# Two constants of a list scheduler, and 64- and 96-row operands of TensorE filled to 128 rows

## The chip, the cores and the metric

One core of a Trainium2 chip runs the program. The metric is the device time of one execution in microseconds; several executions were timed, and one more was recorded by the hardware profiler.

## The reference

Two blocks run one after the other on 512 tokens of width 1024, all in float32. The first has two layers, and each is a feed-forward, a mixer and a feed-forward:

```python
x = x + 0.5 * swiglu(rmsnorm(x, ffn1_norm[l]), ffn1_wg[l], ffn1_wu[l], ffn1_wd[l])
h = rmsnorm(x, mix_norm[l]) @ w_in[l]
h_a, h_b, h_c = jnp.split(h, [A_COLS, A_COLS + B_COLS], axis=-1)
o = jnp.concatenate([mla_mixer(h_a, ...), nsa_mixer(h_b, ...), diff_mixer(h_c, ...)], axis=-1)
x = x + o @ w_out[l]
x = x + 0.5 * swiglu(rmsnorm(x, ffn2_norm[l]), ...)
```

`mla_mixer` has six heads of 64 + 32 channels whose queries and keys come from low-rank factors (192 and 128 wide); the 32 channels are turned by position (rope). `nsa_mixer` has six heads with compressed, selected and windowed keys; its q and three kinds of k get a partial rope. `diff_mixer` has four heads that subtract two softmaxes, with rope on q and k of 32 channels. The second block is a gated recurrence beside a dilated attention, then a mixture of 16 experts, each taking 64 tokens through three 1024x1024 matrices.

## The kernel before

The kernel is not written in the order in which it runs. A `Recorder` takes down every operation with its alternatives (a copy or a small elementwise operation may go to one of two or three engines); a list scheduler then walks through planned time, hands each engine the ready operation of highest priority, gives out the eight PSUM banks, and emits each engine's row of instructions in that order. Its planned lengths come from `duration` (a formula for each engine and operation) and, for TensorE, from `pe`, which goes through the products of one operation and carries `weights`: the last weights, and which 64-column half of the array the last product used. All emitted instructions stand under one line of the profile, L500, so the trace is read by shapes and times.

Float32 accuracy comes from splitting operands into a high and a low float32r part; a product of two such operands is three passes (high x high, high x low, low x high). Loads of weights run on SyncE's queue; splitting the loaded weights is a CAST and a TENSOR_TENSOR of 128x1024 on DVE, ACT or POOL.

A mixer runs in this order as recorded: `group` products for columns "a", then `mla_prep`; the groups "qk", "kv", "cqk" (the differential heads' q and k, 512 columns) and "cv" (their values, 256 columns); `mla_heads`; and then `nsa_prep`, `diff_prep` and the heads of these two. The scheduler mixes them: the large products of the groups fill TensorE while softmaxes of `mla_heads` pass through DVE and ACT, and the ropes of `nsa_prep` run on DVE and POOL. Below, arena_126 is a half of the cv weights as loaded, arena_128 and arena_129 its high and low part; arena_150 and arena_151 are NSA's q and k, arena_153 its doubled k, arena_269 to arena_276 the four terms of a rope, arena_119 and arena_120 the cosine and sine, arena_92 the identity matrix of a transpose.

Operands with fewer than 128 rows are these: `w2l`, the low part of the last 64 rows of the query factor (`mla_prep`, `mla_heads`: 64 rows, where the contraction runs over 64 rows); `QP` and `KP`, the rope channels of MLA as 3 x 32 rows; and `cqk`, the differential heads' q and k, also 3 x 32 rows.

Of the kernel before, what the change touches and what calls it, by code (L numbers as in the profile page):

```python
# [31 lines left out]
       ("ACT", "POOL"): 159, ("DVE", "ACT"): 128, ("DVE", "PE"): 202, ("DVE", "POOL"): 155, ("POOL", "ACT"): 75,  # L32
       ("POOL", "DVE"): 70, ("POOL", "PE"): 149, ("ACT", "ACT"): 34, ("DVE", "DVE"): 127, ("POOL", "POOL"): 102,
       ("PE", "PE"): 0, ("SP", "SP"): 0}
TABLES = {AF.Exp: 1, AF.Silu: 2, AF.Sigmoid: 3, AF.Sin: 4}


# [39 lines left out]
class Recorder:  # L77
# [390 lines left out]
    def pe(self, calls, t, weights):  # L468
        for _, m, a, k in calls:
            out, st, mov = a[0], a[1], a[2]  # L470
            key = (st.tensor.name, st.offset, tuple(st.ap))
            half = out.ap[0][1] == 64 and (out.offset % SPAN) // (512 * 64)
            d = duration("PE", m, a, k)
            if key == weights[0] and st.dtype != F32:
                d = free(mov) / 2.4 + 2.5
            if out.ap[0][1] == 64 and weights[1] is not None and weights[1] == 1 - half:

                d, half = 57, None
            elif out.ap[0][1] != 64:
                half = None  # L480
            t, weights = t + d, (key, half)
        return t, weights
# [35 lines left out]
def duration(eng, m, a, k):  # L518
    aps = [x for x in list(a) + list(k.values()) if is_ap(x)]
    out = k.get("out", a[0] if a else None)  # L520
    if m == "dma_start":
        src = k.get("in_", a[1] if len(a) > 1 else None)
        n = 1
        for c in src.shape:
            n *= c
        return n * 4 / 395.0
    if eng == "PE":
        st, mov = a[1], a[2]
        if m == "transpose":
            return 109.0  # L530
        n, mm = free(mov), free(st)
        if st.dtype == F32:
            return 2 * max(n / 1.2 + 2, 53.0 if mm <= 64 else 107.0)
        return max(n / 2.4 + 2.5, 56.0 if st.dtype == BF else 107.0)
    n = max(free(x) for x in aps)
    ps = any(x.space == PSUM for x in aps)
    if eng == "ACT":
        d = (51 if ps else 93) + 0.834 * n
        if m == "activation":
            d += 93 * (is_ap(k.get("scale")) or is_ap(k.get("bias"))) + 93 * ("accum_out" in k)  # L540
        return d
    if eng == "DVE":
        if m in ("tensor_copy", "memset"):
            return 65 + 1.042 * n if ps else 69 + 0.52 * n
        if m in ("tensor_scalar", "tensor_scalar_mul", "tensor_scalar_add"):
            return (65 + 1.042 * n if ps else 69 + 0.52 * n) + 60 * any(is_ap(x) for x in a[2:])
        if m == "scalar_tensor_tensor":
            return 73 + 1.157 * n
        if m == "reciprocal":
            return 69 + 6.25 * n  # L550
        return 68 + 1.042 * n
    if m in ("memset", "iota", "affine_select"):
        return 100 + 0.834 * n
    if m == "tensor_scalar":
        return 243 + 46 * sum(is_ap(x) for x in a[2:]) + 0.834 * n
    if m == "tensor_scalar_mul":
        return 260 + 3.33 * n
    if m == "tensor_copy":
        return 121 + 3.33 * n
    return 126 + 2.123 * n  # L560
# [62 lines left out]
T = 512  # L623
# [10 lines left out]
def r32(ap):  # L634
    return ap.bitcast(F32R)
# [228 lines left out]
class Mixer:  # L864
# [145 lines left out]
    def tr4(self, src, pool, bufs=2):  # L1010
# [5 lines left out]
            self.nc.tensor.transpose(ps[:r, 128 * c:128 * c + 128], p, self.ident)  # L1016
        return ps[:r]

    def three(self, x):

        return f32(x.rearrange("p a b -> p (a b)"))
# [82 lines left out]
    def mla_prep(self, l, ap, pr, pp, ha):  # L1104
# [10 lines left out]
            q(wkv[:, :768].rearrange("p (h r c) -> p h r c", h=6, r=2)[:, :, r], ukv[:, :, :64])  # L1115
        q(wkv[:, 768:].rearrange("p (h c) -> p h c", h=6), ukv[:, :, 64:])
        w1h, w2h, wkvh = (ap.tile([128, n], F32R, name=m) for m, n in (("w1h", 576), ("w2h", 576), ("wkvh", 1152)))
        w1l, w2l, wkvl = r32(w1), r32(w2[:64]), r32(wkv)
        self.split_sb(w1h, w1l, w1)
        self.split_sb(wkvh, wkvl, wkv)  # L1120
        self.copy(w2h, w2)
        self.tt("tensor_sub", w2l, w2[:64], f32(w2h[:64]))
        sc = 96 ** -0.5

        ss, rr = (ap.tile([128, 2, 4], F32, name=n) for n in ("ss", "rr"))
# [10 lines left out]
        hl = pr.tile([128, 4, 3, 32], F32R, name="kst")  # L1136
        self.copy(hl[:, :, :2], kpe[:, :, None].to_broadcast([128, 4, 2, 32]))
        self.tt("tensor_sub", hl[:, :, 2], kpe, f32(hl[:, :, 0]))
        KP = ap.tile([96, T], F32R, name="KP")
        self.copy(KP, self.tr4(lambda c: self.three(hl[:, c]), pp))  # L1140
        for tb in range(4):
            self.scaled(ha[:, tb, :192], ha[:, tb, :192], rr[:, 0, tb:tb + 1])
            self.scaled(ha[:, tb, 192:320], ha[:, tb, 192:320], rr[:, 1, tb:tb + 1])
# [13 lines left out]
        for c2_ in range(2):  # L1157
            ps = pp.tile([128, T], F32, name="s", bufs=2)
            for c in range(2):
                tok = slice(128 * (2 * c2_ + c), 128 * (2 * c2_ + c) + 128)  # L1160
                out, r = ps[:, 192 * c:192 * c + 192], slice(384, 576)
                for n, (x, w) in enumerate(((c1h, w1h), (c1h, w1l), (c1l, w1h), (c2, w2h), (c2[:64], w2l))):
                    mm(out, x[:, tok], w[:, r], start=c == 0 and n == 0, stop=n == 4, skip_group_check=True)
            self.scaled(qpe[:, 2 * c2_:2 * c2_ + 2], ps[:, :384].rearrange("p (c h d) -> p c h d", c=2, h=6), sc)
        self.rope(qpe, 6, 16, pr)
# [13 lines left out]
    def mla_heads(self, e, mp, pp, oa):  # L1179
# [4 lines left out]
        for p in range(3):  # L1184
            ps = pp.tile([128, T], F32, name="pq", bufs=1)
            w = lambda n: e[n][:, 128 * p:128 * p + 128]
            for n, (a, x) in enumerate((("w1h", "c1h"), ("w1h", "c1l"), ("w1l", "c1h"), ("w2h", "c2"), ("w2l", "c2"))):
                mm(ps, w(a), e[x][:64] if n == 4 else e[x], start=n == 0, stop=n == 4)
            Q = [self.stack2(mp, ps, x, "Q", 2, sc) for x in range(2)]
            passes = []  # L1190
            for x in range(2):
                h = 2 * p + x
                ps = pp.tile([128, T], F32, name="pq", bufs=1)
                for n, (a, c) in enumerate((("wkvh", "ch"), ("wkvh", "cl"), ("wkvl", "ch"))):
                    mm(ps, e[a][:, 128 * h:128 * h + 128], e[c], start=n == 0, stop=n == 2)
                KH, KL, QP = (mp.tile([r, T], F32R, name=n, bufs=2) for n, r in (("KH", 128), ("KL", 128), ("QP", 96)))
                self.split_out(KH, KL, ps)
                ps = self.tr4(lambda c: self.three(e["hq"][:, c, h]), pp)
                self.copy(QP, ps)
                passes.append([(Q[x], KH), (Q[x], KL), (QP, e["KP"])])  # L1200
            av = pp.tile([128, T], F32, name="av", bufs=2)
            for i in (3, 2, 1, 0):
                pt = self.turned(st, [self.softmax(st, i, passes[x]) for x in range(2)], i + 1)
                self.outputs(av, i, i + 1, pt, lambda x, j: e["V"][:, j, 2 * p + x, :], i == 3, True)
            self.split_out(*oa[p], av)
# [28 lines left out]
    def diff_heads(self, l, lam, hl, V, dp, mp, pp, oc):  # L1234
# [4 lines left out]
        for p in range(2):  # L1239
            passes = []  # L1240
            for h in (2 * p, 2 * p + 1):
                w = []
                for c in range(2):
                    qk = []
                    for s in range(2):
                        t = mp.tile([96, T], F32R, name="cqk", bufs=8)
                        self.copy(t, self.tr4(lambda tb: self.three(hl[s][:, tb, 2 * h + c]), pp))
                        qk.append(t)
                    w.append([tuple(qk)])
                passes.append(w)  # L1250
# [942 lines left out]
```

## Time and profile before

| what | value |
|---|---|
| median of 3 executions | 2970.51 us (2967.53 to 2972.78) |
| the profiled execution's own time | 2972.06 us |
| its span in the trace | 2970.3 us |
| mean granted TensorE clock | 0.993 of full speed |
| PE busy | 2894.5 us, 97% |
| DVE, ACT, POOL busy | 56%, 21%, 9% |

The span runs from the first to the last recorded instruction; the profiled execution's own time has 1.8 us around it. The stages on the time axis are: first feed-forward to about 365 us; first mixer 365 to 745; two feed-forwards 745 to 1412; second mixer 1412 to 1790; last feed-forward to 2090; the second block's mixer to about 2490; the experts from there to the end.

### The profile page before, as it was taken

How to read it: one execution, taken by the hardware profiler on the slowest of the kernel's cores; microseconds unless marked ns; L12 is line 12 of the kernel's file. 1: busy time of each engine (PE TensorE's matmuls, PEld its weight loads, DVE VectorE, ACT ScalarE, POOL GpSimd, SP SyncE). 2: the span in 40 equal slices, each digit the busy share in tenths (PEclk: the TensorE clock that was granted, in tenths of full speed). 3: DMA queues.
4: the chain of work that ended last, by engine and by line, in shares of the span. 5: the costliest groups of instructions: out<-in, count | busy, mean ns of one | idle time of the engine just before them, and what ended most of it. 6: DMA issues, size and time to landing. Idle time of an engine off the chain costs nothing.

```text
span 2970.3 us, 37457 instructions
## 1 busy us (share of the span) xinstructions
PE 2894.5 (97%) x14909; PEld 2192.1 (74%) x14909; DVE 1669.2 (56%) x3051; ACT 634.0 (21%) x1364; POOL 279.2 (9%) x279
## 2 busy tenths in 40 slices
PE   9999999999999999999999999999999999999998
PEld 7888877777888888888777778888777876444443
DVE  6554565886555455555658865555767783311212
ACT  3000133472000010001334721001222361100000
POOL 1000111211000010001112210000223120000000
PEclk9999999999999999999999999999999999999999
DMA  4333322102333333333221023333312356999999
GB/s 124 99 93 98 109 78 62 47 5 77 90 100 99 97 89 100 100 96 112 78 60 56 2 78 90 95 96 100 89 57 71 100 179 242 384 409 409 409 409 349
DMA packets 273139, 403.61 MB, mean 136 GB/s; under 512 B 34809, under 2 KB 210982, under 8 KB 272966
## 3 DMA queue, kind: packets, MB, share of 16 engines
q1 hardware_dynamic: 272806, 401.09, 40.1%
q8 instruction: 117, 1.92, 0.3%
q14 instruction: 56, 0.46, 0.0%
q0 software_dynamic: 160, 0.14, 0.0%
HBM read 399.09 MB, written 2.10 MB: 135 GB/s over the span
## 4 chain that ended last, share of the span: by engine, by line
PE 87%; DVE 8%; DMA 3%; issue 1%; ACT 1%; POOL 1%; SPq 0%; DVEq 0%; POOLq 0%; ACTq 0%
PE bank L500 87%; DVE arena L500 8%; DMA arena<-in_w_expert_up 1%; ACT arena L500 1%; DMA arena<-in_ffn_wd 1%; POOL arena L500 1%; DMA arena<-in_w_expert_down 0%; DMA arena<-in_x 0%; SPq L500 0%; DMA arena<-in_w_in 0%; DVEq L500 0%; DVEq L2189 0%; POOLq L500 0%; ACTq L500 0%
## 5 line engine op out<-in xcount | busy, mean ns | idle before, releaser
L500 PE MATMUL bank<-arena 128*128 128x512 f32 (+7 forms) x14909 | 2894.5, 383 | 71.7 <-DVE arena L500 40.5
L500 PEld LDWEIGHTS bank<-arena 128*128 128x128 f32 (+4 forms) x14681 | 2183.4, 176 | 751.9 <-issue 257.5
L500 DVE TENSOR_TENSOR arena<-arena 128x1024 fp32r<-128x1024 f32 (+11 forms) x889 | 689.5, 793 | 33.2 <-PE bank L500 9.1
L500 DVE CAST arena<-arena 128x1024 fp32r<-128x1024 f32 (+6 forms) x394 | 258.9, 658 | 629.4 <-PE bank L500 446.5
L500 POOL TENSOR_TENSOR arena<-arena 128x512 f32<-128x512 f32 (+13 forms) x159 | 206.6, 1306 | 1793.9 <-DVE arena L500 870.3
L500 ACT ACTIVATE arena<-arena 128x512 f32<-128x512 f32 (+4 forms) x313 | 189.2, 627 | 867.1 <-DVE arena L500 729.7
L500 ACT ACTIVATE arena<-bank,arena 128x256 f32<-128x256 f32 (+7 forms) x349 | 177.9, 534 | 452.5 <-PE bank L500 240.5
L500 DVE TENSOR_TENSOR arena<-arena,bank 128x512 f32<-128x512 f32 (+2 forms) x226 | 142.6, 668 | 103.4 <-PE bank L500 97.6
L500 ACT CAST arena<-arena 128x512 fp32r<-128x512 f32 (+3 forms) x94 | 74.5, 798 | 510.6 <-DVE arena L500 424.6
L500 ACT COPY arena<-bank 128x512 f32<-128x512 f32 (+5 forms) x194 | 102.8, 542 | 329.4 <-PE bank L500 324.6
L500 DVE TENSOR_TENSOR arena<-bank,arena 128x512 f32<-128x512 f32 (+3 forms) x207 | 135.2, 676 | 67.1 <-PE bank L500 50.0
L500 DVE SCALAR_TENSOR_TENSOR arena<-bank,arena 128x512 fp32r<-128x512 f32 (+5 forms) x71 | 46.6, 662 | 166.7 <-ACT arena L500 84.7
L500 DVE TENSOR_REDUCE arena<-bank 128x1 f32<-128x256 f32 (+3 forms) x208 | 97.5, 482 | 30.4 <-PE bank L500 27.2
L500 DVE TENSOR_SCALAR arena<-bank,arena 128x128 f32<-128x128 f32 (+5 forms) x88 | 32.4, 411 | 124.7 <-PE bank L500 124.4
L500 DVE TENSOR_SCALAR arena<-arena 128x512 f32<-128x512 f32 (+13 forms) x260 | 87.5, 358 | 17.4 <-ACT arena L500 12.3
L500 DVE COPY arena<-bank 128x512 f32<-128x512 f32 (+8 forms) x91 | 46.7, 514 | 85.2 <-PE bank L500 84.4
L500 DVE SCALAR_TENSOR_TENSOR arena<-arena 128x512 fp32r<-128x512 f32 (+8 forms) x162 | 86.5, 538 | 7.0 <-DMA arena<-in_attn_k_norm_w 4.3
L500 POOL TENSOR_SCALAR arena<-arena 128x512 f32<-128x512 f32 (+3 forms) x93 | 61.9, 668 | 295.2 <-DVE arena L500 259.7
L500 ACT CAST arena<-bank 128x512 fp32r<-128x512 f32 (+2 forms) x99 | 56.0, 577 | 94.8 <-PE bank L500 81.4
L500 ACT ACTIVATION_READ_ACCUMULATOR arena<-bank,arena 128x1 f32 x208 | 42.7, 205 | 0.0
L500 DVE RECIPROCAL arena<-arena 128x1 f32<-128x1 f32 (+2 forms) x249 | 38.0, 162 | 5.6 <-ACT arena L500 4.7
L500 PEld LDWEIGHTS <-arena 128*128 128x128 bf16 x228 | 21.4, 99 | 21.9 <-issue 15.1
(32 smaller groups left out, 157.6 us busy)
## 6 DMA issues: line engine op xcount, KB each, us to landing
arena<-in_w_expert_gate SPq DMA_DIRECT2D x64, 1024.0 KB
arena<-in_w_expert_up SPq DMA_DIRECT2D x64, 1024.0 KB
arena<-in_w_expert_down SPq DMA_DIRECT2D x62, 1024.0 KB
arena<-in_ffn_wg SPq DMA_DIRECT2D x88, 512.0 KB
arena<-in_ffn_wu SPq DMA_DIRECT2D x88, 512.0 KB
arena<-in_ffn_wd SPq DMA_DIRECT2D x80, 512.0 KB
arena<-in_w_in SPq DMA_DIRECT2D x36, 512.0 KB
arena<-in_w_in SPq DMA_DIRECT2D x32, 256.0 KB
```

The costliest lines, as they stand in the source:

```text
L500: last[i] = getattr(getattr(self.real, eng), m)(*a, **k).ins
```

## The change

The planner's cost of a float32r product goes from n/2.4 + 2.5 ns to n/2.4 + 13.4 ns for n streamed columns (512 columns: 215.8 to 226.7 ns). A planned product gets 93 ns more where it writes 64 partitions and `weights[1]` is None, or the reverse; the old discount for equal weights goes. The second product of a pair of 64-column halves sets `weights[1]` to None, so the next pair counts as a change too. These are numbers in the plan; what they change in the program is the order of instructions, the choice of engine and of bank.

The other part changes operands. `blank` copies zeros into the rows beyond the used ones with a POOL instruction, and the tiles get 128 rows. Per layer that is one 64x576 and eleven 32x512 copies (KP, QP for the first two heads, eight `cqk` tiles); 24 in the program. The products then contract over 128 rows: 14 products of 64 rows (six of 512 columns, eight of 192) and 112 products of 96 rows become products of 128.

```diff
+SWITCH = 93
...
             d = duration("PE", m, a, k)
-            if key == weights[0] and st.dtype != F32:
-                d = free(mov) / 2.4 + 2.5
+            if weights[0] is not None and (out.ap[0][1] == 64) != (weights[1] is not None):
+                d += SWITCH
             if out.ap[0][1] == 64 and weights[1] is not None and weights[1] == 1 - half:
...
-        return max(n / 2.4 + 2.5, 56.0 if st.dtype == BF else 107.0)
+        return max(n / 2.4 + 2.5, 56.0) if st.dtype == BF else max(n / 2.4 + 13.4, 107.0)
...
+    def blank(self, t, a):
+
+        self.nc.gpsimd.tensor_copy(t[a:], self.zero[a:].to_broadcast([128 - a, t.shape[1]]))
...
-        w1l, w2l, wkvl = r32(w1), r32(w2[:64]), r32(wkv)
+        w1l, w2l, wkvl = r32(w1), r32(w2), r32(wkv)
...
-        self.tt("tensor_sub", w2l, w2[:64], f32(w2h[:64]))
+        self.tt("tensor_sub", w2l[:64], w2[:64], f32(w2h[:64]))
+        self.blank(w2l, 64)
...
-        KP = ap.tile([96, T], F32R, name="KP")
-        self.copy(KP, self.tr4(lambda c: self.three(hl[:, c]), pp))
+        KP = ap.tile([128, T], F32R, name="KP")
+        self.blank(KP, 96)
+        self.copy(KP[:96], self.tr4(lambda c: self.three(hl[:, c]), pp))
...
-                for n, (x, w) in enumerate(((c1h, w1h), (c1h, w1l), (c1l, w1h), (c2, w2h), (c2[:64], w2l))):
+                for n, (x, w) in enumerate(((c1h, w1h), (c1h, w1l), (c1l, w1h), (c2, w2h), (c2, w2l))):
...
-                mm(ps, w(a), e[x][:64] if n == 4 else e[x], start=n == 0, stop=n == 4)
+                mm(ps, w(a), e[x], start=n == 0, stop=n == 4)
...
-                KH, KL, QP = (mp.tile([r, T], F32R, name=n, bufs=2) for n, r in (("KH", 128), ("KL", 128), ("QP", 96)))
+                KH, KL, QP = (mp.tile([r, T], F32R, name=n, bufs=2) for n, r in (("KH", 128), ("KL", 128), ("QP", 128)))
...
-                self.copy(QP, ps)
+                if h < 2:
+                    self.blank(QP, 96)
+                self.copy(QP[:96], ps)
...
-                        t = mp.tile([96, T], F32R, name="cqk", bufs=8)
-                        self.copy(t, self.tr4(lambda tb: self.three(hl[s][:, tb, 2 * h + c]), pp))
+                        t = mp.tile([128, T], F32R, name="cqk", bufs=8)
+                        if p == 0:
+                            self.blank(t, 96)
+                        self.copy(t[:96], self.tr4(lambda tb: self.three(hl[s][:, tb, 2 * h + c]), pp))
```

The order of instructions moves through the whole program. Three places in the first mixer follow; the second mixer has the same ones.

On PE, before, the last products of group cqk (512 columns, arena_132 and arena_106) run straight into the first of group cv (256 columns).

```order
L500 MATMUL bank4_62<-arena_137,arena_105 128x512
L500 MATMUL bank3_61<-arena_137,arena_105 128x512
L500 MATMUL bank2_60<-arena_132,arena_106 128x512
L500 MATMUL bank0_58<-arena_132,arena_106 128x512
L500 MATMUL bank4_62<-arena_132,arena_106 128x512
L500 MATMUL bank3_61<-arena_132,arena_106 128x512
L500 MATMUL bank7_65<-arena_128,arena_105 128x256
L500 MATMUL bank6_64<-arena_128,arena_105 128x256
L500 MATMUL bank1_59<-arena_128,arena_105 128x256
L500 MATMUL bank7_65<-arena_129,arena_105 128x256
```

On PE, after, cv's products (256 columns) are what stands between the last softmaxes and the transposes of NSA's q (arena_150), followed by the first products of w_out with MLA's outputs (arena_250 to arena_255) and the transposes of NSA's k (arena_151).

```order
L502 MATMUL bank2_60<-arena_92,arena_150 128x128
L502 MATMUL bank5_63<-arena_92,arena_150 128x128 x4
L502 MATMUL bank6_64<-arena_132,arena_106 128x256
L502 MATMUL bank7_65<-arena_132,arena_106 128x256
L502 MATMUL bank1_59<-arena_132,arena_106 128x256
L502 MATMUL bank4_62<-arena_132,arena_106 128x256
L502 MATMUL bank0_58<-arena_250,arena_128 128x512
L502 MATMUL bank0_58<-arena_251,arena_128 128x512
L502 MATMUL bank0_58<-arena_250,arena_135 128x512
L502 MATMUL bank0_58<-arena_252,arena_128 128x512
L502 MATMUL bank6_64<-arena_250,arena_128 128x512
L502 MATMUL bank3_61<-arena_92,arena_151 128x128 x4
```

The cv products began at row 2199 of PE in the changed order, ahead of the last MLA softmaxes; before, they began at row 2232, behind the whole of group cqk.

On DVE, before, the splits of the cv weights (CAST and TENSOR_TENSOR of arena_126) stand behind the rope of NSA's k and doubled k (arena_151, arena_153).

```order
L500 TENSOR_TENSOR arena_270<-arena_151,arena_120 128x64
L500 TENSOR_TENSOR arena_271<-arena_151,arena_120 128x64
L500 TENSOR_TENSOR arena_272<-arena_151,arena_119 128x64
L500 TENSOR_TENSOR arena_276<-arena_153,arena_119 128x128
L500 TENSOR_TENSOR arena_151<-arena_269,arena_270 128x4x2x8
L500 TENSOR_TENSOR arena_268<-arena_267,arena_115 128x24
L500 TENSOR_TENSOR arena_153<-arena_273,arena_274 128x4x4x8
L500 TENSOR_TENSOR arena_151<-arena_271,arena_272 128x4x2x8
L500 TENSOR_TENSOR arena_255<-bank7_65,arena_254 128x512
L500 TENSOR_TENSOR arena_153<-arena_275,arena_276 128x4x4x8
L500 CAST arena_128<-arena_126 128x1024
L500 TENSOR_TENSOR arena_129<-arena_126,arena_128 128x1024
```

On DVE, after, the same splits stand about 60 rows earlier, behind the splits of the cqk weights.

```order
L502 CAST arena_128<-arena_134 128x1024
L502 TENSOR_TENSOR arena_135<-arena_134,arena_128 128x1024
L502 CAST arena_132<-arena_136 128x1024
L502 TENSOR_TENSOR arena_137<-arena_136,arena_132 128x1024
L502 CAST arena_128<-arena_126 128x1024
L502 TENSOR_TENSOR arena_129<-arena_126,arena_128 128x1024
L502 TENSOR_SCALAR arena_152<-bank6_64,arena_165 128x256
L502 TENSOR_SCALAR arena_152<-bank6_64,arena_169 128x256
```

And the end of the rope of NSA's q and k on DVE, after, now comes behind the last softmaxes of MLA; the last term for k (arena_151) is the last row here.

```order
L502 TENSOR_TENSOR arena_153<-arena_275,arena_276 128x4x4x8
L502 TENSOR_TENSOR arena_150<-arena_269,arena_270 128x4x2x8
L502 TENSOR_TENSOR arena_273<-arena_153,arena_119 128x128
L502 TENSOR_TENSOR arena_150<-arena_271,arena_272 128x4x2x8
L502 TENSOR_TENSOR arena_269<-arena_151,arena_119 128x64
L502 TENSOR_TENSOR arena_270<-arena_151,arena_120 128x64
L502 TENSOR_TENSOR arena_271<-arena_151,arena_120 128x64
L502 TENSOR_TENSOR arena_272<-arena_151,arena_119 128x64
L502 TENSOR_TENSOR arena_274<-arena_153,arena_120 128x128
L502 TENSOR_TENSOR arena_151<-arena_269,arena_270 128x4x2x8
L502 TENSOR_TENSOR arena_255<-bank2_60,arena_254 128x512
L502 TENSOR_TENSOR arena_151<-arena_271,arena_272 128x4x2x8
```

From the last scaling of a softmax row (row 495 on DVE) to that last term there are 27 DVE instructions: 25 of rope, one of 128x512 and one of 128x24.

On POOL, after, five of the new copies of zeros (arena_94 is the zero tile) stand together just ahead of rope terms of NSA.

```order
L502 TENSOR_SCALAR arena_228<-arena_228,arena_243 128x256
L502 CAST arena_333<-arena_94 32x512
L502 TENSOR_TENSOR arena_323<-arena_152,arena_120 128x128
L502 CAST arena_335<-arena_94 32x512
L502 CAST arena_339<-arena_94 32x512
L502 CAST arena_341<-arena_94 32x512
L502 CAST arena_337<-arena_94 32x512
L502 TENSOR_TENSOR arena_271<-arena_150,arena_120 128x64
L502 TENSOR_TENSOR arena_272<-arena_150,arena_119 128x64
```

Before, the same place held TENSOR_SCALARs of the softmaxes (arena_238, arena_228) and no copies of zeros.

```order
L500 TENSOR_SCALAR arena_238<-arena_238,arena_240 128x384
L500 TENSOR_SCALAR arena_228<-arena_228,arena_243 128x256
L500 TENSOR_SCALAR arena_238<-arena_238,arena_240 128x384
L500 TENSOR_TENSOR arena_270<-arena_150,arena_120 128x64
L500 TENSOR_TENSOR arena_272<-arena_150,arena_119 128x64
L500 TENSOR_TENSOR arena_271<-arena_150,arena_120 128x64
L500 TENSOR_TENSOR arena_275<-arena_153,arena_120 128x128
L500 TENSOR_SCALAR arena_238<-arena_238,arena_249 128x128
```

## Rows read from the trace of the kernel before

**Rows 1.** The page's head and part 1: busy us, share of the span, instructions.

```profile
span 2970.3 us, 37457 instructions
PE 2894.5 (97%) x14909; PEld 2192.1 (74%) x14909; DVE 1669.2 (56%) x3051; ACT 634.0 (21%) x1364; POOL 279.2 (9%) x279
```

**Rows 2.** What PE waited for, whole span: total, times, longest.

```profile
PE bank L500 <- DVE arena L500: 40.5, 55, 2.6
PE bank L500 <- DMA arena<-in_w_expert_up: 4.6, 4, 1.5
PE bank L500 <- DMA arena<-in_w_expert_down: 3.5, 4, 1.6
```

**Rows 3.** Stages: length, busy by engine, PE clock, DMA share, GB/s.

```profile
365.00:745.00 380.00, 363.63 (x2279) 287.82 (x2278) 272.86 (x646) 161.00 (x418) 71.38 (x79) 0.99 0.19 55
745.00:1412.00 667.00, 665.30 (x2941) 550.04 (x2939) 358.76 (x456) 56.35 (x89) 23.02 (x15) 1.00 0.33 98
1412.00:1790.00 378.00, 362.58 (x2272) 287.50 (x2273) 271.85 (x645) 160.50 (x417) 71.53 (x79) 0.99 0.19 55
...
2550.00:2820.00 270.00, 268.14 (x1411) 125.78 (x1412) 52.58 (x105) 23.64 (x42) 0.00 (x0) 1.00 1.02 404
2820.00:2970.00 150.00, 135.78 (x691) 60.31 (x689) 27.76 (x56) 12.70 (x22) 0.00 (x0) 1.00 0.97 380
```

**Rows 4.** PE's waits in the second mixer, 1412 to 1790 us.

```profile
PE bank L500 <- DVE arena L500: 10.8, 13, 2.6
```

**Rows 5.** Timeline of PE, 523 to 529 us, idle before in brackets.

```profile
522.71 1.29 PE L500 MATMUL bank<-arena 128*128 128x512 f32 x5
526.59 0.62 PE L500 MATMUL bank<-arena 128*128 128x256 f32 x3 [2.58 <-DVE arena L500]
527.85 1.34 PE L500 MATMUL bank<-arena 128*128 128x256 f32 x9 [0.64 <-DVE arena L500]
```

**Rows 6.** Timeline of DVE, 508 to 530 us.

```profile
511.53 13.60 DVE L500 TENSOR_TENSOR arena<-arena 128x64 f32<-128x64 f32 x30
525.05 0.68 DVE L500 TENSOR_TENSOR arena<-bank,arena 128x512 fp32r<-128x512 f32 x1
...
525.85 0.68 DVE L500 CAST arena<-arena 128x1024 fp32r<-128x1024 f32 x1
```

**Rows 7.** Groups by form in 511 to 516 us: busy, mean ns.

```profile
L500 POOL TENSOR_TENSOR arena<-arena 128x1024 f32<-128x1024 f32 x2 | 4.8, 2382 | 0.7 <-DMA arena<-in_nsa_phi_k 0.4 <-DMA arena<-in_nsa_phi_v 0.3
L500 DVE TENSOR_TENSOR arena<-arena 128x64 f32<-128x64 f32 x2 | 3.8, 1924 | 0.0
```

**Rows 8.** Groups by form in 521 to 525.2 us.

```profile
L500 DVE TENSOR_TENSOR arena<-arena 128x64 f32<-128x64 f32 x9 | 2.0, 253 | 0.0
```

**Rows 9.** Short windows between starts of products, columns as in 3.

```profile
454.49:455.87 1.38, 1.38 (x7) 1.12 (x6) 0.00 (x0) 0.00 (x0) 0.00 (x0) 1.00 0.00 0
452.71:454.49 1.78, 1.78 (x8) 1.04 (x6) 0.80 (x2) 0.23 (x1) 0.41 (x1) 1.00 0.00 0
430.36:431.28 0.92, 0.92 (x5) 0.57 (x4) 0.00 (x0) 0.90 (x2) 0.00 (x0) 1.00 0.00 0
412.88:414.90 2.02, 2.02 (x12) 1.42 (x10) 0.75 (x1) 1.15 (x2) 0.00 (x0) 1.00 0.00 0
413.62:413.85 0.23, 0.23 (x4) 0.23 (x3) 0.00 (x0) 0.23 (x1) 0.00 (x0) 1.00 0.00 0
456.56:457.81 1.25, 1.25 (x12) 0.72 (x11) 0.79 (x2) 0.00 (x0) 0.00 (x0) 1.00 0.56 82
457.04:457.26 0.22, 0.22 (x7) 0.22 (x6) 0.22 (x1) 0.00 (x0) 0.00 (x0) 1.00 0.94 121
```

**Rows 10.** Weight loads by form: busy, mean ns.

```profile
L500 PEld LDWEIGHTS bank<-arena 128*128 128x128 f32 x11386 | 1955.6, 186 | 491.8 <-issue 53.7 <-DVE arena L500 51.9 <-ACT arena L500 26.6
...
L500 PEld LDWEIGHTS bank<-arena 96*128 96x128 f32 x112 | 21.4, 194 | 3.0 <-ACT arena L500 1.6 <-issue 0.7
```

**Rows 11.** GpSimd's copy with a change of type, by form.

```profile
L500 POOL CAST arena<-arena 128x896 fp32r<-128x896 f32 x2 | 2.4, 1220 | 10.8 <-PE bank L500 10.8
```

## The prediction

> **What bounds the kernel now.** I read the head of the profile first: TensorE (PE) is busy 2894.5 of 2970.3 us, DVE 56% and POOL 9% [rows 1]. So PE is the bound, and only two things can move the time: the length of PE's own work, and the 75.8 us (2970.3 - 2894.5) in which it stands. The waits of the whole span come next: DVE is behind 40.5 us in 55 pieces of at most 2.6 us; the transfers of the expert weights are behind 4.6 and 3.5 us [rows 2]. The table of stages says where a gain can reach the end. The two feed-forwards between the mixers have 1.7 us without PE in 667 (667.00 - 665.30), so reordering has nothing to win there. Each mixer leaves 15 to 16 us open (380.00 - 363.63, 378.00 - 362.58). The experts run with a DMA share of 1.02 and 404 GB/s from 2550 on and 0.97 after 2820 [rows 3]: there the transfers end last, and a PE that becomes a microsecond faster or slower inside that stage waits a microsecond more or less. What happens before 2490 us moves the end, because it moves the moment from which the expert stage runs.
>
> The second mixer repeats the first: 10.8 us behind DVE, the longest 2.6 [rows 4]. So one mixer is worked out and doubled.
>
> **The padded products.** I price a product by the distance between starts, with windows whose edges are starts (the x counts also take in what drains at an edge, so I count starts in the order). Six products of 128x512 take 1.38 us, 0.231 each. Six of which one has 64 rows take 1.78, so the 64-row product costs 0.40 more, its two neighbours included. Nine products of 192 columns, three with 64 rows, take 2.02; two plain ones take 0.23, nine of these would take 1.04, so a 64-row product costs (2.02 - 1.04) / 3 = 0.33. Four products of 512 columns of which the last two have 96 rows take 0.92, that is 0.231 each: 96 rows cost nothing more than 128 [rows 9]. The loads say the same (194 ns for 96 rows, 186 for 128) [rows 10]; so the 112 products of 96 rows give nothing, 0 from both sides. The 14 of 64 rows give, per layer, 3 x 0.40 + 4 x 0.33 = 2.5 us.
>
> Against this stand two losses that the order shows. The 64-row products and transposes of `nsa_prep` are split into two more groups per layer than before, each an excursion to 64 rows and back: 2 x 0.37 (between 0.33 and 0.40) = 0.7. And the groups of products with 64 output columns rise by about 1.5 per layer. Such a group of four between two of 512 columns takes 1.25 us where two plain 512s (0.46) and four 64-column products (two take 0.22, so 0.44) make 0.90: 0.35 an excursion [rows 9], so 0.5 per layer. Net: -2.5 + 0.7 + 0.5 = **-1.3 us per layer, -2.6 in the two**. The ends are -5.0 (the two losses are nothing) and 0 (twice the losses).
>
> In the experts the order holds some six more 64-column groups, 6 x 0.35 = 2.1 us of PE. I take 0 of it, since the transfers cover it; without that cover it is +2.1.
>
> **The wait that goes.** The largest stall of a mixer is where PE goes from group cqk to group cv. It ends five products and stands 2.58 us, then 0.64 us more, both times for DVE [rows 5]. DVE was at a block of 30 small rope operations, 13.60 us long, and behind that at a 128x512 product; the CAST of the cv weights starts at 525.85, and PE starts 0.74 us later [rows 6]. In the new order the splits of these weights are 60 rows earlier on DVE, ahead of the last softmaxes, and the cv products are spread from row 2199 on. So the 2.58 + 0.64 = 3.22 us go, in each mixer. I find nothing that excludes this.
>
> **The wait that may come.** The rope must be done some time, and now stands behind the last softmaxes. What is late next are the transposes of NSA's q and k. From the last scaling of a softmax (row 495 on DVE) to the last rope term of k there are 27 DVE operations. The 25 of rope cost 0.253 us each when POOL is quiet [rows 8], 6.3 in all; or 13.60 / 30 = 0.45 as in the block of before [rows 6], 11.3. With the 128x512 product (0.68 [rows 6]) and a small one taken at 0.25, they are 7.3 to 12.3 us. In the same stretch, from the transposes of that softmax to those of k, PE has 53 products of 256 columns (half of 0.231, 6.1 us), 5 of 512 (1.2), 12 transposes and 6 short ones (0.11 each, half of the 0.22 [rows 9], 2.0): 9.3 us. So PE waits between nothing (7.3 is less than 9.3) and 3.0 us. I take the middle of 0 and 3.0, 1.5: POOL's large products come in this stretch again, but not all of the block is beside them. The two waits together are -3.2 + 1.5 = -1.7 per layer, with ends -3.2 and -0.2; **-3.4 in both layers**, ends -6.4 and -0.4.
>
> **The copies of zeros.** There are 24 on POOL. A POOL cast of 128x896 takes 1.22 us [rows 11]; by columns a 512-column one is 0.70, so 24 are 17 us, at most 29 if the columns mattered nothing. POOL is busy 279.2 us of 2970.3 [rows 1], and the scheduler takes more work than this off it; most tiles are blanked long before a product reads them. I take 0. Without that cover it is the second rival.
>
> DVE gets about 30 more and ACT some more of the small operations that POOL lost; DVE has 273 of 380 us in the mixer [rows 3]. I take 0 for that outside the stretch above, and 1 us either way.
>
> **The sum.** -2.6 - 3.4 = -6.0 us by these two terms. Part of the moved order is not followed row by row: 15 us of small waits in each mixer sit on other pairs of instructions, and the search that chose the new order did not see real waits. I charge 1 us a mixer for what this puts back, a choice, with 0 and 2 as ends. That makes -4.0. Against the profiled execution's 2972.06 us (1.8 around its span) it is 2968.1; this execution is 1.5 us above the median of 2970.51, so for a median I say **2966.5 us**. The likeliest case alone goes from 2962 to 2972.
>
> **Rivals.** (a) *The stall goes and nothing comes back.* For it speaks that at 0.253 us an operation DVE is ready before PE. Then -2.6 - 6.4 = -9.0, or up to -5.0 - 6.4 = -11.4 with the better end of the padding: 2959 to 2962, about **2961**. Against it speaks the 0.45 of the block before.
>
> (b) *POOL holds DVE in the rope, and the kernel gets slower.* Two 128x64 operations of DVE took 1924 ns on average while POOL was at 128x1024 products of 2382 ns [rows 7]; later the same form took 253 [rows 8]. So an operation of DVE beside one of POOL can last as long as the latter. Five copies of zeros now stand on POOL at the start of the rope, 5 x 0.70 = 3.5 us. If DVE loses all of it behind the last softmaxes, the new wait is 3.0 + 3.5 = 6.5 instead of 1.5 per layer, and with -3.2 and -1.3 a layer is 2.0 us slower; with the losses of the padding doubled (0 instead of -1.3) 3.3, and with the 2.1 us of the experts uncovered the whole is +6.1 to +8.7: about **2978**. It decides from a new wait of about 4.5 us per layer on (3.2 + 1.3). Against it: the copies wait for nothing but a free tile and may be over before the softmaxes end.
>
> The Trainium skill ("SBUF — State Buffer", section "SBUF: two separate sides") speaks of an exclusive lock on a port pair that DVE and GpSimd share, kept for a whole instruction, while the loser stands. The 1924 ns agree with it. By that rule every one of the 24 copies can stop DVE once, and not only the five; this would be 17 us of DVE, most of it where PE doesn't wait for DVE.
>
> (c) *The waits only change place.* The 6.0 us won at the two places come back in small waits on other pairs of instructions, 3 us a mixer of the 15 that stand open there: **2970.5**, no change that can be told. The plan's new lengths differ from the old by 11 ns in 216, and most stages are already without gaps; this speaks for it.
>
> **How the numbers follow.** A measurement of this kernel can tell about 0.2%, 6 us, from no change. The forecast case has 0.42, (a) 0.28, (b) 0.15, (c) 0.15. Faster by over 0.2% means below 2964.6: all of (a) but a little and a fifth of the forecast case, 0.26 + 0.09 = 0.35. Slower, above 2976.4: two thirds of (b) and a little of (c), 0.13. Same: 0.52. The range runs from 2959, the bulk of (a), to 2976, just short of (b): what is left out is a tenth at either end.
>
> **What the profile would show.** Right: no 64x512 and 64x192 products with `w2l`; windows of such a place at 0.231 and 0.115 us a product; no wait of 2.58 us ahead of the first 256-column products in either mixer; a wait of 1 to 3 us at transposes of NSA's q or k some 10 us later; the feed-forward stages unchanged to 0.5 us; the expert stage of the same length at 404 GB/s. Wrong: a wait for DVE over 4 us there, 128x64 operations of DVE beside 32x512 casts of POOL with means over 0.5 us, more waits for ACT in the second block's mixer (2090 to 2490, which I did not work out and took at nothing), or an expert stage that starts its full transfer rate later though the mixers got shorter.

## The result: 0.8% slower, and the profile after

The changed kernel takes 2994.18 us (median of 4, 2993.59 to 2996.07) against 2971.65 for the kernel before in the same session; the ratio is 1.0083, interval 1.0071 to 1.0095. A gain of 4 us was forecast; 23 us were lost.

The head of the profile after, its part 1, and the transfer rate in 40 slices of the span (part 2):

```profile
span 2994.4 us, 37418 instructions
PE 2900.6 (97%) x14909; PEld 2200.7 (73%) x14909; DVE 1673.1 (56%) x3082; ACT 640.5 (21%) x1376; POOL 255.6 (9%) x260
...
GB/s 123 99 95 100 107 73 58 50 4 83 92 97 97 102 92 94 97 99 108 77 59 50 4 83 93 98 96 102 78 54 72 111 197 190 393 409 409 409 409 334
```

The same rate line of the kernel before:

```profile
GB/s 124 99 93 98 109 78 62 47 5 77 90 100 99 97 89 100 100 96 112 78 60 56 2 78 90 95 96 100 89 57 71 100 179 242 384 409 409 409 409 349
```

PE's busy time rose by 6.1 us and the time in which it stands from 75.8 to 93.8 us [rows 1]. Its mean granted clock was 0.991 where it was 0.993. By these means some 12 us more of the span are at the lower level (1.2 GHz), which can explain 6 us of the loss at the most (an estimate from the two means). In the rate line the slices ahead of the four 409s had 179, 242 and 384, and have 197, 190 and 393 now: in the second of them the transfers moved less, and the full rate comes later. What PE waits for:

```profile
PE bank L502 <- DVE arena L502: 49.0, 44, 6.0
PE bank L502 <- ACT arena L502: 18.3, 25, 2.7
PE bank L502 <- DMA arena<-in_w_expert_up: 7.6, 11, 1.3
...
PE bank L502 <- POOL arena L502: 5.0, 3, 3.7
```

DVE is behind 49.0 us in place of 40.5, the longest wait is 6.0 and no longer 2.6 [rows 2], and ACT is behind 18.3 in place of 13.2. The stages that answer to those of before (their edges moved with the program), in the columns of [rows 3]; the last row is the 40 us from the first expert product on:

```profile
365.00:748.00 383.00, 363.19 (x2280) 291.08 (x2281) 277.60 (x662) 163.27 (x422) 64.22 (x72) 0.98 0.19 55
...
1416.00:1794.50 378.50, 359.40 (x2271) 288.59 (x2272) 275.66 (x661) 160.93 (x419) 64.26 (x72) 0.98 0.19 55
...
1794.50:2095.00 300.50, 300.07 (x1324) 248.13 (x1323) 162.65 (x205) 27.99 (x45) 4.50 (x3) 1.00 0.32 97
2513.30:2553.30 40.00, 40.00 (x207) 16.55 (x208) 11.05 (x25) 4.84 (x8) 0.00 (x0) 1.00 0.58 231
```

Two rows of the kernel before, for stages not shown ahead of the prediction; the second is again the 40 us from its first expert product on:

```profile
2090.00:2490.00 400.00, 384.75 (x2130) 312.19 (x2128) 294.00 (x587) 137.31 (x248) 83.79 (x80) 0.98 0.35 116
2499.70:2539.70 40.00, 40.00 (x208) 16.83 (x209) 8.34 (x18) 4.93 (x8) 0.00 (x0) 1.00 0.84 316
```

The share of the loss by stage is read from the starts of products that have the same number in PE's order in both programs. Each program has 12847 products; the 2062 that are plain float32 and no transposes leave two records each, which makes the trace's 14909.

| from product to product | before, us | after, us | difference |
|---|---|---|---|
| 1570 to 3560, first mixer | 381.4 | 383.7 | +2.3 |
| 3560 to 6490, two feed-forwards | 666.9 | 667.9 | +0.9 |
| 6490 to 8470, second mixer | 378.3 | 378.8 | +0.5 |
| 9800 to 11499, second block's mixer | 387.0 | 395.7 | +8.7 |
| 11535 to 12840, the experts | 471.2 | 481.5 | +10.3 |

So four fifths of the loss are in the second block, where not one padded product stands. In its mixer PE waits 9.9 us more. Before (2090 to 2490 us) and after (2095 to 2503):

```profile
PE bank L500 <- DVE arena L500: 11.9, 15, 2.2
PE bank L500 <- POOL arena L500: 2.8, 2, 2.5
```

```profile
PE bank L502 <- DVE arena L502: 16.5, 16, 2.2
PE bank L502 <- POOL arena L502: 5.0, 3, 3.7
PE bank L502 <- ACT arena L502: 3.1, 3, 1.6
```

The waits for ACT, none before, are one of the signs that the prediction named for being wrong. The mixers of the first block, on which the prediction was built, come out nearly even, since a gain and a loss meet there. The wait at the cv weights is gone, as forecast. The wait at the transposes of NSA's q is there, larger. PE first, then DVE:

```profile
524.82 8.64 PE L502 MATMUL bank<-arena 128*128 128x128 f32 x84
539.41 5.88 PE L502 MATMUL bank<-arena 128*128 128x128 f32 x29 [5.95 <-DVE arena L502]
```

```profile
526.39 0.28 DVE L502 TENSOR_SCALAR arena<-arena 128x128 f32<-128x128 f32 x1
526.58 12.17 DVE L502 TENSOR_TENSOR arena<-arena 128x64 f32<-128x64 f32 x25
538.68 0.68 DVE L502 TENSOR_TENSOR arena<-bank,arena 128x512 fp32r<-128x512 f32 x1
```

PE worked until 533.46 us and then stood 5.95; the 25 rope operations took 12.17 us. The last term of q had ended at 536.9. What PE still waited for is the 128x512 product: it empties the bank (bank2_60) into which the next transpose of q writes, and it stands behind the rope in DVE's order. While PE stood, its granted clock fell to 0.50, the lower level (1.2 GHz), from 536.4 to 543.2 us; so PE's first 3.8 us after the wait ran at that level too. POOL's share in these 12 us, in the groups of 530 to 535 us:

```profile
L502 DVE TENSOR_TENSOR arena<-arena 128x64 f32<-128x64 f32 x4 | 4.5, 1187 | 0.0
L502 POOL TENSOR_TENSOR arena<-arena 128x1024 f32<-128x1024 f32 x2 | 4.3, 2174 | 0.0
```

The mean of 1187 ns mixes two kinds: two of the four operations took 0.21 us, and two 1.93 and 2.40 us, each beside a POOL product of 128x1024 and ended 0.1 us after it. With one of 128x128 (1.99 us) these are three operations that took 6.3 us, where their forms take 0.7 with POOL at small work; so 5.6 of the 12.17 us stand beside three POOL products. The kernel before has such products too [rows 7], and 253 ns with POOL at small work [rows 8]. The copies of zeros have little part in it, as POOL's own timeline shows: five had ended at 517.7 us (one stood alone at 510.92), and one more lies at the end of the block, where a 128x64 operation of DVE took 0.63 us beside it.

```profile
510.92 0.61 POOL L502 CAST arena<-arena 32x512 fp32r<-32x512 f32 x1 [4.93 <-PE bank L502]
515.43 2.29 POOL L502 CAST arena<-arena 32x512 fp32r<-32x512 f32 x4 [0.97 <-PE bank L502]
...
527.77 4.02 POOL L502 TENSOR_TENSOR arena<-arena 128x1024 f32<-128x1024 f32 x2 [1.55 <-DMA arena<-in_nsa_phi_k]
...
537.99 0.69 POOL L502 CAST arena<-arena 32x512 fp32r<-32x512 f32 x1
```

The start of the experts is the other place. SyncE issues the transfers of the expert weights, each into a slot of a ring that PE must have left. Its timeline near the first experts, before and then after:

```profile
2479.41 0.37 SPq L500 DMA_DIRECT2D arena<-in_w_expert_up  x1
2504.27 0.88 SPq L500 DMA_DIRECT2D arena<-in_w_expert_down  x2
2510.69 0.88 SPq L500 DMA_DIRECT2D arena<-in_w_expert_gate  x2
2515.84 0.88 SPq L500 DMA_DIRECT2D arena<-in_w_expert_down  x2
2521.41 0.88 SPq L500 DMA_DIRECT2D arena<-in_w_expert_gate  x2
```

```profile
2492.57 0.40 SPq L502 DMA_DIRECT2D arena<-in_w_expert_up  x1
2528.99 1.17 SPq L502 DMA_DIRECT2D arena<-in_w_expert_down  x2
2530.71 1.02 SPq L502 DMA_DIRECT2D arena<-in_w_expert_gate  x2
2535.86 0.88 SPq L502 DMA_DIRECT2D arena<-in_w_expert_down  x2
```

Before, the queue stands 24.4 us between the issue at 2479.41 and the next at 2504.27; after, 36.0 us from 2492.57 to 2528.99. PE's first expert products start at 2499.7 and 2513.3, so the first slots come free 4.5 us after that before, and 15.7 us after that now: a slot is half a weight tile, and four products read it. Before, ten products with the first pair of tiles stand together, and the last of the four that the first issue waits for starts at 2503.2. In the new order six stand together, and PE then goes to other tiles and, from 2523 us on, round four pairs by turns; the last of the four starts at 2527.9. In the 40 us from the first expert product on the transfers therefore run at 231 GB/s, where they ran at 316. The 3.4 MB that this leaves behind take 8.3 us at 409 GB/s, most of the 10.3.

The two direct parts of the change did what they should. Six products of 512 columns, the third of them with w2l and now of 128 rows:

```profile
414.83:416.22 1.39, 1.39 (x7) 1.13 (x6) 1.15 (x2) 0.66 (x2) 1.04 (x1) 1.00 0.00 0
```

That is 1.39 us, 0.232 a product, as for plain ones [rows 9]. And the copies of zeros by form (the forecast had 0.70 us for one):

```profile
L502 POOL CAST arena<-arena 32x512 fp32r<-32x512 f32 x22 | 15.2, 704 | 23.7 <-PE bank L502 22.0 <-DVE arena L502 1.2
L502 POOL CAST arena<-arena 64x576 fp32r<-64x576 f32 x2 | 2.4, 1206 | 2.3 <-ACT arena L502 2.3
```

### The profile page after: what moved, and what is told of

Read it like the earlier page. It is cut to its first block, busy times and chain, and to the rows that moved or that the text cites. A ratio compares the mean times of both kernels' runs of the same rounds, so it can differ in the third digit from the quotient of the medians.

```text
span 2994.4 us, 37418 instructions
## 1 busy us (share of the span) xinstructions
PE 2900.6 (97%) x14909; PEld 2200.7 (73%) x14909; DVE 1673.1 (56%) x3082; ACT 640.5 (21%) x1376; POOL 255.6 (9%) x260
## 4 chain that ended last, share of the span: by engine, by line
PE 82%; DVE 9%; DMA 6%; ACT 1%; issue 1%; POOL 0%; SPq 0%; DVEq 0%; ACTq 0%; POOLq 0%
PE bank L502 82%; DVE arena L502 9%; DMA arena<-in_w_expert_up 4%; ACT arena L502 1%; DMA arena<-in_w_expert_gate 1%; DMA arena<-in_ffn_wd 1%; POOL arena L502 0%; DMA arena<-in_w_expert_down 0%; SPq L502 0%; DMA arena<-in_x 0%; DMA arena<-in_ffn_wu 0%; ACT L502 0%; DVEq L502 0%; DVEq L2201 0%; ACTq L502 0%
## 5 line engine op out<-in xcount | busy, mean ns | idle before, releaser
L502 PE MATMUL bank<-arena 128*128 128x512 f32 (+9 forms) x14909 | 2900.6, 383 | 89.0 <-DVE arena L502 49.0
L502 PEld LDWEIGHTS bank<-arena 128*128 128x128 f32 (+2 forms) x14681 | 2192.4, 176 | 768.8 <-issue 250.3
L502 DVE TENSOR_TENSOR arena<-arena 128x1024 fp32r<-128x1024 f32 (+14 forms) x907 | 694.0, 784 | 51.6 <-PE bank L502 22.4
L502 DVE CAST arena<-arena 128x1024 fp32r<-128x1024 f32 (+4 forms) x396 | 258.4, 653 | 615.2 <-PE bank L502 448.4
L502 ACT ACTIVATE arena<-arena 128x512 f32<-128x512 f32 (+5 forms) x319 | 192.2, 626 | 852.3 <-DVE arena L502 716.4
L502 POOL TENSOR_TENSOR arena<-arena 128x512 f32<-128x512 f32 (+12 forms) x141 | 180.4, 1284 | 1793.1 <-ACT arena L502 775.3
L502 ACT ACTIVATE arena<-bank,arena 128x512 f32<-128x512 f32 (+6 forms) x346 | 176.6, 536 | 487.5 <-DVE arena L502 286.5
L502 ACT CAST arena<-arena 128x512 fp32r<-128x512 f32 (+5 forms) x92 | 73.7, 805 | 501.2 <-DVE arena L502 412.8
L502 DVE TENSOR_SCALAR arena<-arena 128x512 f32<-128x512 f32 (+14 forms) x279 | 97.4, 372 | 14.9 <-ACT arena L502 10.2
L502 ACT CAST arena<-bank 128x512 fp32r<-128x512 f32 (+3 forms) x103 | 57.8, 581 | 125.3 <-PE bank L502 103.7
L502 PEld LDWEIGHTS <-arena 128*128 128x128 bf16 x228 | 20.4, 98 | 19.8 <-issue 13.4
```

The costliest lines, as they stand in the source:

```text
L502: last[i] = getattr(getattr(self.real, eng), m)(*a, **k).ins
```

## The experiments

"Length" is the planned length of a float32r product of 512 columns. Times are medians. The runs were made in four groups, each with its own runs of the kernel before (2969.79, 2970.47, 2969.12 and 2971.18 us); a ratio is to those. My first theory, A: the loss is in the order that the charge of 93 ns for a switch makes. Rivals: B, the operands cost time; C, every new order is drawn at random.

**pad_only.** The changed kernel with both planner numbers set back:

```diff
-            if weights[0] is not None and (out.ap[0][1] == 64) != (weights[1] is not None):
-                d += SWITCH
+            if key == weights[0] and st.dtype != F32:
+                d = free(mov) / 2.4 + 2.5
...
-        return max(n / 2.4 + 2.5, 56.0) if st.dtype == BF else max(n / 2.4 + 13.4, 107.0)
+        return max(n / 2.4 + 2.5, 56.0 if st.dtype == BF else 107.0)
```

> The padding alone, with the planner's numbers of before (the 24 copies of zeros enter the plan, so the order still moves). Theory A (the loss is in the order that the switch cost of 93 ns makes, above all among the experts): 2966 to 2972 us, the 64-row products 2.5 us cheaper per layer, no wait over 3 us at the transposes of NSA's q, expert transfers at full rate from about 2540 us as before. Theory B (operands of 128 rows cost PE time, or the copies of zeros hold DVE): 2985 to 2995 us. Theory C (any new order is drawn anew, the numbers don't matter): anywhere from 2965 to 2995, with the waits at places of its own.

2965.96 us, ratio 0.9992 (0.9982 to 1.0001). B falls: the padding doesn't cost the time that was lost, and its 3.8 us can just not be told from none. Its order is a new one too, so this run alone doesn't price the operands; the windows of products above do. SyncE's wait is 23.9 us.

**plan_only.** The reverse: both planner numbers in the kernel before, no padding.

> Both planner numbers alone, no padding. Theory A: 2992 to 2999 us, 3 to 5 us above the changed kernel because the 64-row products are back, with SyncE standing over 30 us ahead of the expert weights near 2500 us. Theory B: about 2972. Theory C: anywhere from 2965 to 2995.

3003.18 us, ratio 1.0117 (1.0100 to 1.0134), 4 above the range of A. SyncE's wait is 36.0 us, as A had it. The whole loss, and more, is in the plan.

**no_switch** (`SWITCH = 0` in the changed kernel) and **no_len** (13.4 back to 2.5) part the two numbers:

> The changed kernel with a switch cost of 0 instead of 93 ns; padding and the longer float32r products stay. Theory A: 2966 to 2975 us, SyncE's wait near 2500 us back to about 24 us. Theory B: 2990 to 2995. Theory C: anywhere from 2965 to 2995.

> The changed kernel with the old length of float32r products (2.5 ns instead of 13.4 beyond the columns); padding and the switch cost stay. Theory A: 2988 to 2998 us, SyncE's wait near 2500 us still over 30 us. Theory B: 2990 to 2995. Theory C: anywhere from 2965 to 2995.

2982.38 us (1.0042, 1.0028 to 1.0057) and 2980.40 (1.0036, 1.0022 to 1.0049). Each number alone costs 10.6 to 12.6 us over the kernel before; A is missed by both times, above by the one and below by the other; the queue's wait followed A (23.7 us without the switch cost, 34.7 with it). So A was half the story. In the starts of the products they part by place: the longer length lost 6.7 us in 9800 to 10600 (second block's mixer) and 1.1 in the experts; the switch cost lost 1.7 and 5.4.

**pair_state.** As no_len, but a finished pair leaves the state at 64 columns:

```diff
-                d, half = 57, None
+                d, half = 57, 2
```

> Padding, the old product length and the switch cost of 93 ns, but a finished pair of 64-column halves leaves the state at 64 columns, so that the second and later pairs in a row are not charged. Theory S (the loss among the experts comes from charging every pair, 93 ns on 950 planned, where the trace has 858 for a pair): the expert stage as before, SyncE's wait near 2500 us back from 34.7 to about 24 us, 2966 to 2972 in all. Theory C: anywhere from 2965 to 2995, and the wait not tied to it.

2967.18 us (0.9993, 0.9983 to 1.0002), 13 below no_len and in the range of S. (The planner's formula has 914 ns for a pair and 1007 with the charge, not the 950 of the expectation; 0.86 us is what pairs take in the trace.) SyncE's wait went from 34.7 to 27.7 us, not all the way to 24:

```profile
2473.20 0.37 SPq L502 DMA_DIRECT2D arena<-in_w_expert_up  x1
2501.29 0.88 SPq L502 DMA_DIRECT2D arena<-in_w_expert_down  x2
```

The experts' stage is 1.9 us above that of before, no_len's 5.4. This speaks for the charge on every pair, not the charge on a true switch, as what did the harm there; the rest of the 13 us is from other orders ahead of the experts.

**Lengths.** Now theory M: a plan that holds PE's products shorter than they are keeps PE behind its plan, so the others are ready in time. All padded, no switch cost, no discount; the edit is the one number in `n / 2.4 + 13.4`:

```diff
-SWITCH = 93
+SWITCH = 0
...
-        return max(n / 2.4 + 2.5, 56.0) if st.dtype == BF else max(n / 2.4 + 13.4, 107.0)
+        return max(n / 2.4 + 2.5, 56.0) if st.dtype == BF else max(n / 2.4 - 8.0, 107.0)
```

len_short (-8.0), len_old (+2.5), len_long (+24.0), and later len_shorter (-20.0):

> Padding, no switch cost, no discount for equal weights, and a planned float32r product shorter than the trace's (n/2.4 - 8 ns, 205 for 512 columns, where the traces have 227 to 231). Theory M (a plan that holds PE's products shorter than they are keeps PE behind its plan, so that what DVE, ACT and POOL deliver is ready; a plan of the true length has no such margin): 2960 to 2968 us, the second block's mixer no longer than before. Theory C (every new order is drawn anew): anywhere from 2965 to 2995, with no order by length.

> The same with the planned length of before (n/2.4 + 2.5 ns, 216): against the run with the padding alone only the discount for equal weights is gone, which had the same formula. Theory M and theory C: the same order, 2966 us. It tells whether the discount did anything.

> The same with a planned product longer than the trace's (n/2.4 + 24 ns, 237). Theory M: slower than the 2982 us with 13.4 ns, 2985 to 3000, most of it in the second block's mixer. Theory C: anywhere from 2965 to 2995, as likely below 2982 as above.

> Padding, no switch cost, planned product n/2.4 - 20 ns (193 for 512 columns, 15% below the trace's). Theory M: 2938 to 2955 us, with less waiting for DVE than with 216 ns; it must end somewhere, since a plan far too short also orders wrongly. Theory C: 2965 to 2995.

2946.26 (ratio 0.9917, 0.9902 to 0.9932), 2965.78, 2982.52 and 2956.06 us. len_short beats both kernels by more than the changed one lost. The sign is as M has it, short faster and long slower than before, but the sizes aren't: len_short is 14 us below its range, len_long 2 below, no slower than with 13.4 ns, and len_shorter 1 above, slower than len_short. C, which had no time below 2965, misses the two short ones. len_old isn't the order of pad_only, as both theories had it: the discount also let products with the same weights go below the planner's floor of 107 ns, so without it the order differs; the time is the same to 0.2 us. PE's waits for DVE follow the length up to 227 ns; two of the rows, of no_switch (227 ns) and of len_short (205 ns):

```profile
PE bank L502 <- DVE arena L502: 57.8, 50, 5.2
```

```profile
PE bank L502 <- DVE arena L502: 30.1, 32, 2.7
```

**Does the length act without the padding?** before_short is the kernel before with -8.0 and no discount, before_long the same with +13.4:

> The kernel before, without the padding, with a planned float32r product of n/2.4 - 8 ns and no discount. Theory M: the gain of the short length is in the order and not in the operands, so 2948 to 2954 us, some 4 above the padded one with the same length (2946). Theory C: anywhere from 2955 to 2995.

> The kernel before, unpadded, with a planned product of n/2.4 + 13.4 ns, no discount and no switch cost. Theory M: 2982 to 2992 us, PE's waits for DVE over 43 us where the kernel before has 40.5 and the same with the short length 29.4. Theory C: anywhere from 2950 to 2990.

2969.23 us (0.9997, 0.9987 to 1.0006), a miss for M, and 2987.89 (1.0054, 1.0037 to 1.0071), a hit for M that the range of C holds too. So the gain of len_short didn't come again, and the loss of the longer length did. The row of before_long:

```profile
PE bank L498 <- DVE arena L498: 53.9, 49, 6.6
```

**How far does an order scatter?** short_near has -8.5 for -8.0, long_near 13.0 for 13.4:

> As the padded run with n/2.4 - 8 ns (2946 us), with n/2.4 - 8.5 ns. Theory M with little scatter: 2942 to 2952 us. If an order by itself scatters by 10 us or more (theory C): 2955 to 2975, and then no single run of this series says much; PE's waits for DVE tell more, which theory M has at 25 to 31 us, theory C anywhere between 25 and 58.

> As the padded run with n/2.4 + 13.4 ns and no switch cost (2982 us), with n/2.4 + 13.0 ns. Theory M: 2975 to 2988 us, PE's waits for DVE 43 to 58 us. Theory C: anywhere from 2950 to 2985.

2967.49 and 2975.50 us; the waits are 36.0 and 46.5 us. The first is a hit for C and a miss for M by time and wait; the second fits both. So about half a nanosecond in the plan moved the time by 21 us in one case and 7 in the other: C has its part, and the 2946 us of len_short were in part luck.

**Is it margin?** With the true length, DVE's planned times were stretched, by 1.1 in dve_margin and 1.2 in dve_margin2 (`return 1.1 * (68 + 1.042 * n)` and so on):

> Padding, no switch cost, the true product length (n/2.4 + 13.4 ns), and DVE's planned lengths 1.1 times as long. Theory M: the margin can as well stand on the engine that PE waits for, so well below the 2982 us that the true length gives alone: 2950 to 2970. Theory C: 2965 to 2995.

> As the run with DVE's planned lengths 1.1 times as long (2959 us), now 1.2 times. Theory M: 2945 to 2965 us, PE's waits for DVE 25 to 31 us. Theory C: anywhere from 2950 to 2990, waits up to 58 us.

2959.10 (0.9956, 0.9939 to 0.9973) and 2989.90 us (1.0064, 1.0049 to 1.0079). The first agrees with M and lies below the range of C; the second is the reverse: against no_switch PE waits less for DVE (35.1 us, 57.8) but more for ACT (25.8, 6.8), and POOL took over work (348.5 us busy, 257.4), which no run separates further. PE's waits and part 1 of dve_margin2:

```profile
PE bank L502 <- DVE arena L502: 35.1, 35, 3.2
PE bank L502 <- ACT arena L502: 25.8, 34, 2.5
```

```profile
PE 2898.0 (97%) x14909; PEld 2204.3 (74%) x14909; DVE 1625.4 (54%) x2908; ACT 695.7 (23%) x1458; POOL 348.5 (12%) x352
```

**short_pair**, the changed kernel with -8.0 and the pair's state mended:

> The changed kernel with both errors undone: a switch cost of 93 ns that a row of pairs pays once, and a planned product of n/2.4 - 8 ns. If the two parts add: about 2946 to 2950 us, a switch cost so charged being worth little. Theory C: 2965 to 2995.

2958.40 us (0.9956, 0.9941 to 0.9971): better than both kernels, but 8 us above the range in which the two parts add, and 12 above len_short, which is within the scatter of an order.

The runs without a charge on each pair and with DVE's planned lengths unchanged, by the planned length:

| length, ns | time, us | PE's waits for DVE, us |
|---|---|---|
| 193 | 2956 | 24.8 |
| 205 | 2946, 2967 (204.8 ns), 2969 (unpadded), 2958 (pair_state's charge) | 30.1, 36.0, 29.4, 29.7 |
| 216 | 2966, 2966, 2967 (pair_state), 2971 (before) | 38.2, 38.8, 42.2, 40.5 |
| 227 | 2976, 2982, 2988 (unpadded) | 46.5, 57.8, 53.9 |
| 237 | 2983 | 43.3 |

## Why the prediction was wrong, by its steps

**The padded products** (-2.6 us): right in what was measured; the two losses in the sum were not. The products with w2l stand at the distance of plain ones, the 96-row ones gave nothing that shows, and the padding alone measured -3.8 us within an interval that holds -2.6 and 0.

**The copies of zeros at nothing**: right, 15.2 + 2.4 = 17.6 us of POOL for 17 forecast, and pad_only carries them without loss.

**The wait that goes** (-3.2 a mixer): right. In neither mixer does PE now stand more than 0.3 us ahead of a product of 256 columns.

**The wait that may come**, "I take the middle of 0 and 3.0, 1.5": mis-sized. It was 5.95 us in the first mixer and 5.54 in the second. In the first, two terms were off. PE's was the larger: I let it work for 9.3 us, up to the transposes of k, but it already stood at a transpose of q, 6.3 us after the transposes of the last softmax began (527.1 to 533.46), since the bank it writes was not free. DVE took 12.7 us from the last scaling to the end of its 128x512 product (526.7 to 539.36), a little over my upper 12.3; the 1.5 that I took stands for 10.8. The two waits of a mixer so make +2.7 and +2.3 us, not -1.7. Rival (b) had 6.5 for it, by the copies of zeros; the size was near, but what the rows show beside the long operations are POOL's products of 128x1024. That the block would be short without them is not shown by a run.

**The second block's mixer, "which I did not work out and took at nothing"**: the step that failed first. +8.7 us, with 9.9 us more of waits for DVE, POOL and ACT. Its place is tied to the planned length: in 9800 to 10600 all six runs with 227 ns or more and DVE's lengths unchanged are 6.2 to 9.1 us over the kernel before, and all nine others with 216 or less between -5.8 and +3.7.

**The experts, "a PE that becomes a microsecond faster or slower inside that stage waits a microsecond more or less"**: failed, +10.3 us. The 404 GB/s were read as an independent end. But a transfer starts only when PE has left a slot, so PE's order at the first experts decides when the full rate begins. The three runs with 93 ns on every pair lost 10.3, 8.7 and 5.4 us here, the fourteen others at most 3.8. I had counted the new groups as product time, 6 x 0.35 us, and not looked at SyncE's own wait.

**The sum**: the charge of 1 us a mixer for the rest of the moved order was far too small as a range. The order was followed at three places of the first block only, and half a nanosecond of planned length can move 21 us.

What stays open is why a true planned length orders worse than one that is 5 to 15% short. That it does is shown by groups: no run with 227 ns or more and DVE's lengths unchanged is below 2975 us, none at 216 or less without the charge on each pair is above 2972. The two groups nearly touch, with means of 2982 and 2963 us, and inside the lower one the times don't go by length. The margin that I gave as a reason is only argued: dve_margin speaks for it, dve_margin2 against it.

## What to carry to other kernels

A number in a planner that is truer to the trace need not be a better number: its effect is the order that comes out, and that has to be timed with near neighbours of the number beside it, or one lucky or unlucky order is taken for a rule. Where a stage is held by transfers, read the wait of the queue that issues them: who frees the buffers sets when the full rate starts. A change of a plan moves every stage, so work out the ones without a changed operation too, or widen the range by what one order differs from the next.

## What the runs showed of the hardware

A 64-row product of 512 columns between 128-row ones costs 0.40 us more than one of 128 rows, a 96-row one nothing more [rows 9]. DVE operations of 128x64 and 128x128 that take 0.2 to 0.3 us alone lasted 1.9 to 2.4 us beside POOL products of 128x1024 and ended 0.1 us after them. Three of them are 5.6 us, nearly a wait of PE of 6 us.
